# A transformer pair on one core: the low parts of the context stream's weights subtracted on VectorE instead of GpSimd

## The chip, the core and the metric

The kernel runs on one core of a Trainium2 chip. The time is the device time of one execution in microseconds (us). Before the change three runs took 2317.82, 2322.16 and 2325.53 us, a median of 2322.16 us. The kernel is one long program of some 38,000 instructions on five engines: TensorE (PE in the profile; its weight loads are PEld), VectorE (DVE), ScalarE (ACT), GpSimd (POOL) and the queue that issues transfers (SP).

## The reference, cut to what matters

Two model blocks follow each other on 256 tokens of width 1024, batch 1. The first is a mixing block; the second has two layers with a second stream of 256 context tokens. The parts that this case speaks of:

```
def first_block(x, ...):                       # "block 1"
    xn = rms_norm(x, norm_mix); proj = xn @ w_in
    y_r = rwkv7_group(proj[..., :R_COLS], ...)      # a recurrent state over the tokens, 8 heads of 64x64
    y_n = nsa_group(proj[..., R_COLS:], ...)        # sparse attention
    h = x + concatenate([y_r, y_n]) @ w_out
    h = h + swiglu(rms_norm(h, norm_ffn), w_gate, w_up, w_down)
    return rms_norm(h, norm_final)

def second_block(x, c, ctx, c_ctx, w_ada, ...):
    h_x, h_c = x, ctx                               # two streams
    for l in range(2):
        mod_x = silu(c) @ w_ada[l] + b_ada[l]       # the "ada" products; mod_c likewise from c_ctx
        h_x = half_ffn(h_x, ..., ffn1_up[l], ffn1_down[l])
        h_c = half_ffn(h_c, ..., ffn1_up[l], ffn1_down[l])
        ... attention of three kinds over both streams, w_out, a second half_ffn ...
    return rmsnorm(h_x, final_g)
```

The context stream of the second block's first layer (`h_c`) needs nothing of the first block. Its feed-forward part and the ada products can therefore be worked on while block 1 is under way.

## The kernel before, in words

All large products are in float32 by way of two parts. A weight piece of 128x1024 numbers (512 KB) is loaded as `r`. ScalarE casts it to a reduced format, the high part `h` (line 356). A subtraction then gives the low part `l = r - h` (line 357). The activations are held as a high and a low part too (`yh`, `yl`, or `hh`, `hl` inside a feed-forward part). `gemm` adds three products per slice into PSUM: first, for all slices, weight-high times activation-high (line 364) and weight-high times activation-low (line 365), then, for all slices, weight-low times activation-high (line 368). So the low part of a piece is wanted only after 16 products with its high part, in a piece of 8 slices.

The class `Stream` holds the buffers of one such supply of weights: so many raw pieces, so many `h` and `l`. Three of them matter. `s1` and `s` feed block 1 and the main stream. `st_c` (name "sc", 3 raw, 2 `h`, 2 `l`) feeds the context stream: the context's first feed-forward part and then its mixer, and the raw pieces of the ada products (line 1168, which need no parts). Only `st_c` is made with `eng=g`, so only its subtractions run on GpSimd; the others run on VectorE. The tile names tell the streams apart on TensorE: PSUM tiles of the context and ada work are named `f` while block 1 runs, those of block 1 are named `m` and `o`.

Block 1 has long chains of small steps. Those that the prediction speaks of, in order of time: the sparse attention (lines 732 to 796, about 160 to 300 us); the preparation of the recurrence (lines 829 to 926, 300 to 345 us); the products `LT`, `QB`, `AK`, `QK` (lines 951 to 955, to 374 us); a triangular solve written as 31 pairs of dependent VectorE instructions (`tm` at line 977, `TW` at line 978, 374 to 412 us); the recurrence over 8 chunks of tokens (lines 994 to 1055, 423 to 502 us), in which each chunk needs the state `SB` of the one before (L1023, then `U` at L1024, then L1031 and L1032, then the new `SB` at L1041; GpSimd scales the old state at L1040); and the end (lines 1064 to 1085), where a mean, a variance with a power on GpSimd (`hr`, line 855) and a gate follow each other, and then the first pieces of `w1o` are loaded (called "the tail" below).

The order of the instructions on each engine is not written out by hand. The program is built with a scheduler that plays a timeline of its own and puts every engine's instructions into one fixed queue in the order in which that timeline finds them ready. Each engine then works through its queue in order. So the context and ada products are spread between block 1's steps on TensorE by this planner.

Of the kernel before, what the change touches and what calls it, by code (L numbers as in the profile page):

```python
# [15 lines left out]
OP = mybir.AluOpType  # L16
# [249 lines left out]
def build(tc, A, O, dbg=(), stop=None):  # L266
    nc = tc.nc
    v, s, g, te, sy = nc.vector, nc.scalar, nc.gpsimd, nc.tensor, nc.sync
    es = ExitStack()

    def pool(name, bufs=1, space=None, side=None, stack=es, **k):
        if space is not None:
            k["space"] = space
        if side is not None:
            k["side"] = side
        return stack.enter_context(tc.tile_pool(name=name, bufs=bufs, **k))
# [7 lines left out]
    def tl(p, shape, dt=F32, tag="", bufs=None, name=None):  # L284
        k = {}
        if tag:
            k["tag"] = tag
        if bufs:
            k["bufs"] = bufs
        return p.tile(list(shape), dt, name=uniq(name or tag or "t"), **k)  # L290
# [8 lines left out]
    f32 = lambda a: a.bitcast(F32)  # L299
# [31 lines left out]


    class Stream:
        def __init__(self, name, nr, nh, side=None, stack=es, eng=None, parts=None):
            self.nr = nr
            self.raw = pool(name + "r", nr, side=side, stack=stack)
            self.h = pool(name + "h", nh, side=side, stack=parts or stack)
            self.l = pool(name + "l", nh, side=side, stack=parts or stack)
            self.q = sy
            self.e = eng or v  # L340

        def load(self, src, a, b, i=0):

# [8 lines left out]
        def get(self, src, a, b):  # L352
            r = self.load(src, a, b)
            h = tl(self.h, [128, 1024], F32R, tag="h")[:, 0:a * b].rearrange("p (a b) -> p a b", a=a)
            l = tl(self.l, [128, 1024], F32R, tag="l")[:, 0:a * b].rearrange("p (a b) -> p a b", a=a)
            s.copy(h, r)  # L356
            self.e.tensor_tensor(l, r, f32(h), op=OP.subtract)  # L357
            return h, l

    def gemm(pt, w, m0, m1, xs):  # L360
# [1226 lines left out]
    R = "right"  # L1587
# [4 lines left out]

    rs, rs2 = ExitStack(), ExitStack()
    pad = pool("pada", 1, side=R, stack=rs)
    st_c = Stream("sc", 3, 2, side=R, stack=rs, eng=g, parts=rs2)
    st_c.pad = pad
    e = ExitStack()
    first = []
# [89 lines left out]
    rs = ExitStack()  # L1688
# [75 lines left out]
```

## Time and profile before

| what | value |
|---|---|
| runs | 2317.82, 2322.16, 2325.53 us |
| the profiled execution's own time | 2317.79 us |
| its span, first to last instruction | 2315.6 us |
| TensorE busy | 2215.6 us (96%), weight loads 1935.3 us |
| VectorE, ScalarE, GpSimd busy | 1365.0, 965.7, 361.1 us |
| subtractions of line 357 on VectorE | 467, 1233 ns on average |
| subtractions of line 357 on GpSimd | 80, 2431 ns on average, 194.2 us in all |
| mean granted TensorE clock | 0.979 of 2.4 GHz |

The profiled execution took 2317.79 us, 2.2 us more than its span, and 4.4 us less than the median of the runs. TensorE is busy nearly all the time, so the useful reading is where it is not. The 80 subtractions on GpSimd start between 110.5 and 776.0 us of the span.

### The profile page before, as it was taken

To read this page: it belongs to the slowest core of one execution; us is meant where nothing else is said; L and a number is where in the kernel's file an instruction comes from. 1 tells how busy PE (TensorE), PEld (TensorE's weight loads), DVE (VectorE), ACT (ScalarE), POOL (GpSimd) and SP (SyncE) were. 2 spreads that over 40 slices of the span, in tenths; PEclk is the share of its full clock that TensorE was granted. 3 is DMA by queue.
4 is the path that set the end of the run, shared out by engine and by line. 5 is a ranking of instruction groups with operands and counts; after the bars stand their busy time and mean duration, and the time that the engine had idled before them with its cause. 6 is when DMAs were issued, how large, how long until landed. Compare 5 with 4: busy or idle time off the path is not lost.

```text
span 2315.6 us, 38336 instructions
## 1 busy us (share of the span) xinstructions
PE 2215.6 (96%) x15317; PEld 1935.3 (84%) x15317; DVE 1365.0 (59%) x2442; ACT 965.7 (42%) x1602; POOL 361.1 (16%) x286
## 2 busy tenths in 40 slices
PE   7999988998999899998999999999999999989998
PEld 3687876878999799997878777798888889878998
DVE  4465567348665876667765333357534347776665
ACT  4334432226444555445643222245332325564443
POOL 2025464444010300002010000011000002310000
PEclk9999999999999999999999999999999999999999
DMA  8765544436655245554166434376623235413554
GB/s 312 255 220 191 175 159 143 135 121 215 197 183 176 91 129 167 185 168 144 58 221 228 175 131 167 134 236 210 200 87 97 95 119 170 140 46 122 187 183 127
DMA packets 114929, 376.25 MB, mean 162 GB/s; under 512 B 18464, under 2 KB 24480, under 8 KB 114752
## 3 DMA queue, kind: packets, MB, share of 16 engines
q1 hardware_dynamic: 114752, 373.82, 49.1%
q8 instruction: 120, 1.97, 0.3%
q14 instruction: 57, 0.47, 0.1%
HBM read 372.20 MB, written 1.57 MB: 161 GB/s over the span
## 4 chain that ended last, share of the span: by engine, by line
PE 76%; issue 9%; DVE 7%; DMA 4%; POOL 2%; ACT 1%; SPq 0%; POOLq 0%; DVEq 0%; ACTq 0%
PE m L364 13%; PE m L365 13%; PE m L368 13%; PE f L364 8%; PE f L365 7%; PE f L368 7%; PE f L1168 4%; PE o L1399 2%; DVE l L357 1%; PE f L1389 1%; DMA r<-in_up 1%; ACT h L356 1%; DMA r<-in_ada 1%; DVE tm L977 1%; POOL sa L400 1%
## 5 line engine op out<-in xcount | busy, mean ns | idle before, releaser
L356 ACT CAST h<-r 128x1024 fp32r<-128x1024 f32 (+1 forms) x547 | 570.0, 1043 | 950.4 <-PE m L365 453.9
L357 DVE TENSOR_TENSOR l<-r,h 128x1024 fp32r<-128x1024 f32 (+1 forms) x467 | 575.5, 1233 | 284.1 <-ACT h L356 236.7
L365 PE MATMUL m<-yl,h 128*128 128x256 f32 (+1 forms) x1624 | 441.9, 303 | 3.5 <-DVE yl L437 3.4
L364 PE MATMUL m<-yh,h 128*128 128x256 f32 (+1 forms) x1624 | 441.5, 303 | 1.5 <-ACT yh L436 1.5
L364 PEld LDWEIGHTS m<-yh,h 128*128 128x128 f32 x1624 | 310.1, 192 | 27.3 <-issue 10.4
L365 PEld LDWEIGHTS m<-yl,h 128*128 128x128 f32 x1624 | 310.4, 192 | 21.4 <-DVE yl L437 6.4
L368 PE MATMUL m<-yh,l 128*128 128x256 f32 (+1 forms) x1624 | 258.6, 300 | 0.0
L357 POOL TENSOR_TENSOR l<-r,h 128x1024 fp32r<-128x1024 f32 x80 | 194.2, 2431 | 368.2 <-ACT h L356 234.3
L368 PEld LDWEIGHTS m<-yh,l 128*128 128x128 f32 x1624 | 225.1, 190 | 14.2 <-issue 3.7
L400 POOL TENSOR_TENSOR sa<-sa,sq 128x256 f32<-128x256 f32 x81 | 83.3, 1029 | 873.2 <-ACT sq L396 462.9
L365 PE MATMUL m<-hl,h 128*128 128x256 f32 (+1 forms) x738 | 207.0, 303 | 0.0
L364 PE MATMUL m<-hh,h 128*128 128x256 f32 (+1 forms) x738 | 197.2, 304 | 0.0
L364 PE MATMUL f<-yh,h 128*128 128x256 f32 (+1 forms) x624 | 185.3, 321 | 1.1 <-ACT yh L436 1.1
L365 PE MATMUL f<-yl,h 128*128 128x256 f32 (+1 forms) x624 | 184.1, 319 | 0.0
L365 PEld LDWEIGHTS m<-hl,h 128*128 128x128 f32 x738 | 139.8, 189 | 6.9 <-issue 0.4
L364 PEld LDWEIGHTS m<-hh,h 128*128 128x128 f32 x738 | 135.9, 189 | 11.1 <-issue 2.1
L1549 DVE SCALAR_TENSOR_TENSOR res<-m,mod,res 128x256 f32<-128x256 f32 x176 | 81.0, 479 | 108.0 <-PE m L368 105.5
L364 PEld LDWEIGHTS f<-yh,h 128*128 128x128 f32 x624 | 119.2, 191 | 17.3 <-issue 5.4
L364 PE MATMUL f<-hh,h 128*128 128x256 f32 (+1 forms) x446 | 126.6, 313 | 6.5 <-DVE res L1549 6.3
L368 PE MATMUL m<-hh,l 128*128 128x256 f32 (+1 forms) x738 | 129.9, 302 | 0.0
L365 PE MATMUL f<-hl,h 128*128 128x256 f32 (+1 forms) x446 | 126.6, 306 | 2.4 <-DVE hl L372 2.4
L1168 PE MATMUL f<-r,sc 128*32 128x512 f32 (+1 forms) x640 | 118.3, 573 | 8.4 <-DMA r<-in_ada 7.8
(513 smaller groups left out, 3772.5 us busy)
## 6 DMA issues: line engine op xcount, KB each, us to landing
r<-in_up SPq DMA_DIRECT2D x252, 512.0 KB, 3.6
r<-in_ada SPq DMA_DIRECT2D x144, 512.0 KB, 4.4
r<-in_dn SPq DMA_DIRECT2D x98, 512.0 KB, 3.9
r<-in_w1u SPq DMA_DIRECT2D x44, 512.0 KB, 3.5
r<-in_dn SPq DMA_DIRECT2D x32, 448.0 KB, 3.3
r<-in_w2m SPq DMA_DIRECT2D x24, 512.0 KB, 3.8
r<-in_w2o SPq DMA_DIRECT2D x24, 512.0 KB, 3.4
r<-in_w1d SPq DMA_DIRECT2D x22, 512.0 KB, 3.5
```

What stands on the lines that cost most here:

```text
L356: s.copy(h, r)
L357: self.e.tensor_tensor(l, r, f32(h), op=OP.subtract)
L364: te.matmul(pt, w[0][:, k, m0:m1], xs[k][0], start=k == 0, stop=False)
L365: te.matmul(pt, w[0][:, k, m0:m1], xs[k][1], start=False, stop=False)
L368: te.matmul(pt, w[1][:, k, m0:m1], xs[k][0], start=False, stop=k == n - 1)
L400: g.tensor_tensor(acc, acc, sq, op=OP.add)
L977: v.tensor_mul(tm, TW[:, 0:m, j:j + 1].to_broadcast([128, m, n]), Ls[:, j:j + 1, j + 1:32].to_broadcast([128, m, n]))
L1168: te.matmul(pt[j * 32:j * 32 + 32], adac[:, k], w[j], start=k == 0, stop=k == KD - 1)
L1389: te.transpose(pT[:, b * 128:b * 128 + 128], P[:, b * 128:b * 128 + 128], ident)
L1399: te.matmul(po[j * 64:j * 64 + 64], vals(b // 2, b % 2, kvof(2 * pr + j)), PT[j][:, b], start=b == 0, stop=b == nt - 1)
L1549: v.scalar_tensor_tensor(r, pt[:, i * T:i * T + T], ad[l].M[:, m, d, q:q + 1], r, op0=OP.mult, op1=OP.add)
```

## The change

The subtractions of `st_c` are issued on VectorE, like those of the other streams. The argument that chose the engine goes away. No instruction's shape, type or buffer changes; 80 instructions move from GpSimd's queue to VectorE's.

```diff
     class Stream:
-        def __init__(self, name, nr, nh, side=None, stack=es, eng=None, parts=None):
+        def __init__(self, name, nr, nh, side=None, stack=es, parts=None):
             self.nr = nr
...
             self.q = sy
-            self.e = eng or v
...
             s.copy(h, r)
-            self.e.tensor_tensor(l, r, f32(h), op=OP.subtract)
+            v.tensor_sub(l, r, f32(h))
             return h, l
...
-    st_c = Stream("sc", 3, 2, side=R, stack=rs, eng=g, parts=rs2)
+    st_c = Stream("sc", 3, 2, side=R, stack=rs, parts=rs2)
```

Because the planner places instructions by its own timeline, the queues of the engines come out in another order. Lines after 340 have a number lower by one in the changed kernel (L977 and L978 become L976 and L977, L1023 becomes L1022, L357 becomes L356).

VectorE's queue in the middle of the triangular solve (`tm`, `TW`; `res` is the context stream's residual, `fu`, `ft`, `hl` its activations). Before:

```order
L977 TENSOR_TENSOR tm_2226<-TW_2181,Ls_2178 128x7x18
L978 TENSOR_TENSOR TW_2181<-TW_2181,tm_2226 128x7x18
L1549 SCALAR_TENSOR_TENSOR res_60<-f_4398,mod_11_85,res_60 128x256
L977 TENSOR_TENSOR tm_2229<-TW_2181,Ls_2178 128x8x17
L1549 SCALAR_TENSOR_TENSOR res_60<-f_4412,mod_11_85,res_60 128x256
L978 TENSOR_TENSOR TW_2181<-TW_2181,tm_2229 128x8x17
L1549 SCALAR_TENSOR_TENSOR res_60<-f_4432,mod_11_85,res_60 128x256
L977 TENSOR_TENSOR tm_2232<-TW_2181,Ls_2178 128x8x16
L978 TENSOR_TENSOR TW_2181<-TW_2181,tm_2232 128x8x16
L977 TENSOR_TENSOR tm_2235<-TW_2181,Ls_2178 128x9x15
```

The same place on VectorE in the changed kernel:

```order
L356 TENSOR_TENSOR l_4738<-r_4735,h_4737 128x1024
L976 TENSOR_TENSOR tm_2223<-TW_2181,Ls_2178 128x7x19
L371 TENSOR_TENSOR hl_4720<-ft_4717,hh_4719 128x256
L977 TENSOR_TENSOR TW_2181<-TW_2181,tm_2223 128x7x19
L976 TENSOR_TENSOR tm_2226<-TW_2181,Ls_2178 128x7x18
L977 TENSOR_TENSOR TW_2181<-TW_2181,tm_2226 128x7x18
L976 TENSOR_TENSOR tm_2229<-TW_2181,Ls_2178 128x8x17
L458 SCALAR_TENSOR_TENSOR fu_4768<-ft_4766,f_4741 128x256
L977 TENSOR_TENSOR TW_2181<-TW_2181,tm_2229 128x8x17
L976 TENSOR_TENSOR tm_2232<-TW_2181,Ls_2178 128x8x16
L977 TENSOR_TENSOR TW_2181<-TW_2181,tm_2232 128x8x16
L976 TENSOR_TENSOR tm_2235<-TW_2181,Ls_2178 128x9x15
```

Subtractions of weight pieces now stand between the pairs of the solve: 12 between its first and its last instruction, 15 with those just ahead of it and behind it. The context stream is also further on at the same step of the solve: its PSUM tile is `f_4741` here where it was `f_4398` before.

TensorE's queue in one chunk of the recurrence, from the sixth product with the state on (`m`, `o` are block 1's; `f` is the context stream's fill). Before, its first 12 rows; 40 rows lie between the two L1023:

```order
L1023 MATMUL m_2489<-SB_407_1914,WT_2290 32x128 x4
L1026 MATMUL o_2463<-AR_2009,SB_407_1914 128x32 x4
L1031 MATMUL m_2499<-Vt_2078,Kt_2064 128x128
L365 MATMUL f_4984<-ylc_1018,h_4951 128x256
L364 MATMUL f_4984<-yhc_1017,h_4951 128x256
L365 MATMUL f_4984<-ylc_1018,h_4951 128x256
L364 MATMUL f_4984<-yhc_1017,h_4951 128x256
L365 MATMUL f_4984<-ylc_1018,h_4951 128x256
L364 MATMUL f_4984<-yhc_1017,h_4951 128x256
L365 MATMUL f_4984<-ylc_1018,h_4951 128x256
L364 MATMUL f_4984<-yhc_1017,h_4951 128x256
L365 MATMUL f_4984<-ylc_1018,h_4951 128x256
```

The same chunk on TensorE in the changed kernel, whole:

```order
L1022 MATMUL m_2489<-SB_407_1914,WT_2290 32x128 x4
L1025 MATMUL o_2463<-AR_2009,SB_407_1914 128x32 x4
L1030 MATMUL m_2499<-Vt_2078,Kt_2064 128x128
L1031 MATMUL m_2499<-U_2334,Bt_2050 128x128
L1030 MATMUL m_2499<-Vt_2078,Kt_2064 128x128
L1031 MATMUL m_2499<-U_2334,Bt_2050 128x128
L1030 MATMUL m_2499<-Vt_2078,Kt_2064 128x128
L1031 MATMUL m_2499<-U_2334,Bt_2050 128x128
L1030 MATMUL m_2499<-Vt_2078,Kt_2064 128x128
L1031 MATMUL m_2499<-U_2334,Bt_2050 128x128
L1022 MATMUL m_2514<-SB_406_1913,WT_2290 32x128 x4
```

The fill is gone from this chunk. From the first product of line 994 to the first product of `w1o`, TensorE's queue held 296 context products and 32 ada products before, and holds 44 and 16 now; the others stand earlier, 102 and 12 of them in the solve.

## Rows read from the trace of the kernel before

**Rows 1.** The page's busy times: engine, busy us, share, instructions.
```profile
PE 2215.6 (96%) x15317; PEld 1935.3 (84%) x15317; DVE 1365.0 (59%) x2442; ACT 965.7 (42%) x1602; POOL 361.1 (16%) x286
```

**Rows 2.** Busy us (instructions) of PE, PEld, DVE, ACT, POOL by stretch; clock, DMA.
```profile
100.00:300.00 200.00, 194.49 (x1519) 160.24 (x1518) 108.62 (x236) 83.98 (x182) 82.05 (x44) 1.00 0.61 202
300.00:345.00 45.00, 37.73 (x259) 31.93 (x258) 37.40 (x50) 15.00 (x20) 27.77 (x13) 0.92 0.43 142
345.00:374.00 29.00, 29.00 (x168) 20.74 (x166) 16.21 (x39) 5.19 (x8) 10.14 (x6) 1.00 0.54 161
374.00:423.00 49.00, 37.62 (x279) 34.33 (x277) 36.47 (x82) 12.19 (x16) 22.59 (x10) 0.90 0.48 141
423.00:490.00 67.00, 67.00 (x561) 60.15 (x557) 21.75 (x38) 15.45 (x21) 31.10 (x22) 1.00 0.34 114
490.00:531.00 41.00, 33.70 (x240) 23.02 (x240) 22.46 (x42) 11.91 (x23) 19.73 (x15) 0.95 0.54 187
```

**Rows 3.** The same view of three short stretches with a low clock.
```profile
305.00:312.00 7.00, 5.13 (x25) 5.08 (x25) 6.24 (x12) 4.12 (x5) 2.89 (x1) 0.51 0.37 129
390.40:393.90 3.50, 3.50 (x16) 3.50 (x17) 2.48 (x9) 1.04 (x1) 0.23 (x1) 0.51 0.16 63
407.50:414.40 6.90, 5.86 (x27) 5.86 (x28) 3.62 (x17) 1.45 (x2) 0.00 (x0) 0.51 0.34 84
```

**Rows 4.** TensorE's waits, 100 to 423 us: who, for whom, us, times, longest.
```profile
PE f L364 <- DVE res L1549: 8.1, 4, 4.2
PE f L364 <- DVE fu L459: 3.6, 1, 3.6
PE f L365 <- DVE hl L372: 2.4, 1, 2.4
...
PE f L368 <- POOL l L357: 0.3, 1, 0.3
```

**Rows 5.** The page's groups of line 357: busy us, mean ns | idle before, releaser.
```profile
L357 DVE TENSOR_TENSOR l<-r,h 128x1024 fp32r<-128x1024 f32 (+1 forms) x467 | 575.5, 1233 | 284.1 <-ACT h L356 236.7
...
L357 POOL TENSOR_TENSOR l<-r,h 128x1024 fp32r<-128x1024 f32 x80 | 194.2, 2431 | 368.2 <-ACT h L356 234.3
```

**Rows 6.** Line 357 on VectorE: ns min/median/max, first and last start.
```profile
L357 DVE TENSOR_TENSOR l<-r,h x467: 1078/1219/3101, 18.5 to 2294.1; 128x1024 fp32r<-128x1024 f32 x145, 128x896 fp32r<-128x896 f32 x11
```

**Rows 7.** VectorE in order of time in the solve: start us, us.
```profile
382.43 0.28 DVE L977 TENSOR_TENSOR tm<-TW,Ls 128x110 f32<-128x110 f32 x1
...
385.94 2.38 DVE L977 TENSOR_TENSOR tm<-TW,Ls 128x120 f32<-128x120 f32 x1
```

**Rows 8.** GpSimd in order of time, the same stretch (one of 8 rows).
```profile
385.84 2.35 POOL L357 TENSOR_TENSOR l<-r,h 128x1024 fp32r<-128x1024 f32 x1 [0.41 <-DMA r<-in_up]
```

**Rows 9.** TensorE on PSUM tiles `f` alone: stretch, busy us (instructions), clock, DMA.
```profile
423.00:531.00 108.00, 51.58 (x370) 0.98 0.42 142
```

**Rows 10.** A chunk of the recurrence in order of time.
```profile
489.70 1.08 PE L1026 MATMUL o<-AR,SB 128*128 128x32 f32 x8
489.80 0.69 DVE L1024 TENSOR_TENSOR U<-m,Uv 32x512 f32<-32x512 f32 x1 [1.83 <-PE m L1023]
...
494.67 0.38 PE L1032 MATMUL m<-U,Bt 32*128 32x128 f32 x2
...
495.16 0.87 DVE L1041 TENSOR_TENSOR SB<-st,m 64x256 f32<-64x256 f32 x2 [3.94 <-PE m L1032]
...
497.12 1.06 PE L1023 MATMUL m<-SB,WT 128*32 128x128 f32 x8
```

**Rows 11.** The tail in order of time.
```profile
507.32 1.06 ACT L1067 ACTIVATE sq<-Y 128x1024 f32<-128x1024 f32 x1 [2.94 <-DVE Y L1065]
...
511.77 2.90 POOL L855 TENSOR_TENSOR hr<-hr,mhalf 128x16 f32<-128x16 f32 x1 [13.09 <-DVE hr L854]
...
515.45 1.09 PE L864 MATMUL m<-cst,rx 128*128 128x128 f32 x8 [1.45 <-DVE rx L859]
...
530.70 0.58 PE L364 MATMUL m<-mixh,h 128*128 128x256 f32 x1 [5.85 <-ACT h L356]
```

## The prediction

> **What bounds the kernel now.** I read the page's busy times first. TensorE is busy 96% of the span, VectorE 59%, GpSimd 16% [rows 1]. So the time is TensorE's work, which the change leaves as it is, plus the time in which TensorE has nothing to do or runs at half clock. Only that remainder can move.
>
> The second view is the table by stretch. The subtractions that change engine run mostly under block 1, so I cut that part by its stages. TensorE's idle time is the stretch less PE's busy time: 5.5 us in the attention (100 to 300), 7.3 us in the preparation (300 to 345), none in the products (345 to 374), 11.4 us in the solve (374 to 423), none in most of the recurrence (423 to 490) and 7.3 us in its end and the tail (490 to 531) [rows 2]. That is 31.5 us, of which 24.2 us lie before 423.
>
> Third, the clock. Three stretches before 423 run at 0.51 of 2.4 GHz, that is at the 1.2 GHz level, with 5.13, 3.50 and 5.86 us of TensorE work in them [rows 3]. At full clock that work would take about half, so some 7 us are lost there. Idle time and clock together are 31 us before 423: the ceiling of any gain there.
>
> Fourth, the waits of TensorE before 423. It waited 0.3 us for a subtraction on GpSimd, once. It waited 8.1, 3.6 and 2.4 us for VectorE's `res`, `fu` and `hl` of the context stream [rows 4]. So the subtraction itself is hidden. If GpSimd costs anything, it is by what it does to VectorE.
>
> **The price of one subtraction.** On GpSimd it takes 2431 ns on average, 80 times, 194.2 us [rows 5]. On VectorE the same operation takes 1078 ns at best and 1219 ns in the middle [rows 6]. So VectorE gets 80 x 1.08 = 86 us, at most 80 x 1.22 = 98 us. Most of them fall before 531 us.
>
> **What goes: VectorE held by GpSimd.** In the solve `tm` takes 0.28 us at 382.43 and 2.38 us at 385.94, for shapes that differ by 9% [rows 7]. A subtraction on GpSimd runs from 385.84 for 2.35 us [rows 8]. The VectorE instruction that starts inside it ends with it. There are 8 such subtractions in the solve, so about 8 x 2.0 = 16 us of 36.5 us VectorE busy time there is standing still; I count 15, since one of them came too late in its overlap to cost the full amount.
>
> The Trainium skill states this as a rule ("SBUF — State Buffer", section Who interferes with whom): a VectorE instruction with two SBUF inputs and a GpSimd instruction that reads SBUF exclude each other, and the later one waits until the other has finished. The trace agrees, 2.38 us against 0.28 us. But another page ("Perfetto Trace Analysis", section Optimizing Scalar/DVE Operations) warns that, because the two share a port, moving work between them might not help. By it the gain below would be nothing and the sum would be plus 17 us; the rows decide for a gain, since VectorE stands 2.0 us per collision and needs 1.1 us to do the work itself.
>
> **The solve (374 to 423).** VectorE loses 15 us of standing and gains 15 subtractions (front part), 15 x 1.08 = 16 us, and some 4 us more of `fu`, `ft`, `hl`: 36.5 - 15 + 16 + 4 = 42 us. TensorE's queue gains 102 context and 12 ada products there. The 370 recorded fill instructions of 423 to 531 take 51.58 us, 0.14 us each [rows 9], and an ada product of the queue is two of those. So TensorE's work grows from 37.6 to about 37.6 + 14 + 3 = 55 us. Before, VectorE's chain was the longer; now TensorE's work is, by 13 us. I expect its idle time to fall from 11.4 to 4 us, and the clock loss there (4.7 us of the 7) to go: a gain of 12 us. Bounds: 16 us (all of it), and a loss of 4 us if VectorE's queue stalls. A subtraction in VectorE's queue waits for its cast on ScalarE, on average 236.7 / 467 = 0.5 us today [rows 5]; 15 of them are 7.6 us, which fits under the 13 us. What is queued behind such a wait is the solve itself and `res`, `fu`, `hl`, for which TensorE waits.
>
> **The preparation (300 to 345).** VectorE is busy 37.4 of 45 us and GpSimd 27.8 us, which is some ten subtractions [rows 2]. About eight would come to VectorE (9 us) against some 8 us of standing that go. Since `hl` and `res`, for which TensorE waited, are held less, I take a gain of 4 us with the clock, from a loss of 6 to a gain of 8. **The attention (100 to 300)** has 5.5 us idle, and more fill between its steps; I take nothing, from -5 to +4.
>
> **What comes: a recurrence without fill.** The queue behind line 994 holds 44 + 16 fill products where it held 296 + 32. In recorded instructions that is 44 + 32 = 76 of 370, so 294 x 0.14 = 41 us of fill have moved to before 423. Moving costs nothing as such. But the recurrence is a chain, and what hid its waits is gone. In the chunk shown, `U` (0.69 us from 489.80) is hidden by L1026, which ends at 490.78. After the last L1032 (494.67) `SB` takes until 496.03, and L1023 needs it: 495.16 + 0.87 - (494.67 + 0.38) = 1.0 us, with the hand-over 1.2 us [rows 10]. Four of the seven chunks have nothing there now: 5 us (3 to 7). In one chunk two subtractions for the mixer stand in VectorE's queue ahead of `SB`, right after the last ada loads; I add 2 us (0 to 5).
>
> **The tail.** Fill hid the waits for the mean and for `sq` (about 1.5 and 2 us, an estimate: 1.06 us of ScalarE for `sq`, and VectorE steps as wide as `U` with its 0.69 us), and part of the power on GpSimd: `hr` takes 2.90 us, and only 1.45 us of the wait for it showed [rows 11]. Without fill I get 1.5 + 2 + 4 = 7.5 us where 1.45 us showed: a loss of 6 us (3 to 9), and 1 us at the first `w1o` piece, where 5.85 us of waiting for its load remain. More idle time in the tail should bring the half clock there: 3 us (0 to 7). After 531 us TensorE is nearly full, and the moved subtractions there lie under its work; I take nothing.
>
> **The sum.** Gains 12 + 4 = 16 us; losses 5 + 2 + 6 + 1 + 3 = 17 us. On the profiled execution's 2317.8 us that is 2319 us; on the median of the runs, 4.4 us higher, 2323 us. With every term at its better end it would be 22 us faster (gains 16 + 8 + 4, losses 3 + 0 + 3 + 0 + 0); with every term at its worse end 44 us slower (4 + 6 + 5, and 7 + 5 + 9 + 1 + 7). They will not all fall on one side.
>
> **The rivals.** First, **the locks pay in full**: VectorE answers sooner in every stretch before 423, and TensorE's 31 us there shrink to about 12, while the recurrence and the tail cost 10. That is 9 to 15 us faster, 2307 to 2313 us. For it: all the large waits of TensorE there name VectorE [rows 4]. Against: fill that is used early is missing later.
>
> Second, **VectorE's queue becomes the bound**: subtractions stand in it in a fixed place and wait for casts, which wait for loads and for TensorE to free the two `h` buffers; each of about 40 of them in the attention, the preparation and the solve holds it for 0.5 us beyond its own 1.08 us, so 20 us of waits, half of them in chains that TensorE waits for. It decides where VectorE was already full, at 300 to 345. That takes 10 us off the gain, and with the losses it is 10 to 20 us slower, 2333 to 2343 us. Against: VectorE has 59% load overall [rows 1]. The warning of the page "Perfetto Trace Analysis" in the Trainium skill, read as no gain at all, comes to a time in the same range.
>
> Third, **nothing happens**, because TensorE never waited for GpSimd's subtraction: 2322 us. Against: the queues do change, by hundreds of rows.
>
> **How the numbers follow.** A measurement here tells about 0.3% (7 us) from no change. Forecast (the sum) 0.35, nothing happens 0.09, locks in full 0.27, queue the bound 0.29. The forecast and the third rival lie within 0.3%: 0.44 same; 0.27 faster, 0.29 slower. The forecast's own range is 2316 to 2330 us. The range for 8 in 10 takes in most of both other cases: 2307 to 2340 us.
>
> **What would show it.** Right: no VectorE `tm` over 1 us; TensorE idle under 6 us in the solve; 1 us of idle time per late chunk of the recurrence, which takes about 60 us instead of 79; 13 us or more idle in the tail. Wrong: idle time of TensorE before 423 that stays above 24 us, with waits for `l` or for `res` behind an `l`; or a tail that shows no more waiting than before.

## The result: slower, by 0.7 to 0.8%

Four runs of the changed kernel took 2336.8, 2338.68, 2340.07 and 2345.07 us, a median of 2339.38 us against 2323.27 us for the kernel before: a ratio of 1.0076 (95% interval 1.0050 to 1.0102). Timed again later beside other kernels (e16 below) it was 1.0068 (1.0055 to 1.0081). The forecast of 2323 us, no change that can be measured, was wrong; the time fell at the far end of the range.

The profiled execution took 2340.07 us. The page's busy times, the group of line 356 (357 before) and the mean clock, to be held against [rows 1, 5]:

```profile
PE 2232.3 (95%) x15317; PEld 1951.7 (83%) x15317; DVE 1389.8 (59%) x2522; ACT 967.3 (41%) x1602; POOL 167.8 (7%) x206
...
L356 DVE TENSOR_TENSOR l<-r,h 128x1024 fp32r<-128x1024 f32 (+1 forms) x547 | 667.5, 1221 | 337.7 <-ACT h L355 289.7 <-PE m L367 17.7 <-PE f L367 9.9
...
core 0: 2338.3 us, clock 0.969
```

VectorE has the 80 subtractions at 1.22 us each and is hardly busier (1389.8 us against 1365.0, where 80 x 1.22 us make 98), because GpSimd no longer makes it stand still. But TensorE, with the same 15317 instructions, is busy 16.7 us longer. Work that is the same and takes longer is a matter of the clock: 0.969 here, 0.979 before.

The table by stretch says where; columns as in [rows 2], cut at the changed kernel's own stages (preparation, solve, then from the first product of line 993 on, with a cut where the clock fell and one at the end of the recurrence):

```profile
320.00:366.00 46.00, 39.67 (x295) 34.72 (x294) 39.13 (x61) 16.91 (x25) 7.84 (x3) 0.93 0.51 179
...
391.00:444.50 53.50, 49.04 (x405) 44.39 (x404) 40.68 (x102) 19.70 (x26) 0.00 (x0) 0.97 0.64 206
444.50:483.90 39.40, 36.31 (x322) 30.42 (x322) 14.30 (x28) 5.29 (x8) 4.37 (x8) 1.00 0.43 148
483.90:521.40 37.50, 32.72 (x148) 26.72 (x145) 6.86 (x13) 0.58 (x1) 3.02 (x5) 0.50 0.05 15
521.40:546.00 24.60, 16.02 (x47) 9.55 (x46) 11.93 (x22) 6.62 (x14) 10.34 (x11) 0.57 0.13 48
```

The solve's idle time is 53.5 - 49.0 = 4.5 us where it was 11.4. But from 483.9 to 546 us TensorE runs almost throughout at the 1.2 GHz level (0.50 and 0.57); in the same stages before, the table showed 1.00 and 0.95 [rows 2]. Just before the clock fell at 483.9 us it had waited 3.02 us, because two subtractions of the mixer's weights stood in VectorE's queue ahead of the new state `SB`:

```profile
480.10 2.53 DVE L356 TENSOR_TENSOR l<-r,h 128x1024 fp32r<-128x1024 f32 x2 [4.91 <-ACT h L355]
...
482.66 0.87 DVE L1040 TENSOR_TENSOR SB<-st,m 64x256 f32<-64x256 f32 x2
...
483.68 1.68 PE L1022 MATMUL m<-SB,WT 128*32 128x128 f32 x8 [3.02 <-DVE SB L1040]
```

The place is not fixed. In another profiled execution of the same kernel (e16, its slowest, 2351.1 us) the clock was low already in the first chunk, from 449.3 us on: 0.57 from 449.2 to 474.4 us, with TensorE busy throughout. What TensorE waited for in the first execution between 444 and 548 us (who, for whom, us, times, longest):

```profile
PE m L1022 <- DVE SB L1040: 6.4, 4, 3.0
PE m L863 <- DVE rx L858: 4.1, 1, 4.1
PE f L422 <- DVE sq L420: 2.3, 1, 2.3
PE m L848 <- ACT sq L1066: 2.0, 1, 2.0
PE m L1063 <- DVE Y L1054: 1.4, 1, 1.4
```

One whole chunk of the recurrence in order of time, the answer to [rows 10]:

```profile
492.33 1.89 PE L1022 MATMUL m<-SB,WT 128*32 128x128 f32 x8 [1.12 <-DVE SB L1040]
494.15 1.92 PE L1025 MATMUL o<-AR,SB 128*128 128x32 f32 x8
494.26 0.68 DVE L1023 TENSOR_TENSOR U<-m,Uv 32x512 f32<-32x512 f32 x1 [2.07 <-PE m L1022]
...
499.14 0.63 PE L1031 MATMUL m<-U,Bt 32*128 32x128 f32 x2
499.88 0.87 DVE L1040 TENSOR_TENSOR SB<-st,m 64x256 f32<-64x256 f32 x2 [4.94 <-PE m L1031]
...
500.90 1.46 PE L1022 MATMUL m<-SB,WT 128*32 128x128 f32 x6 [1.12 <-DVE SB L1040]
```

The wait for `SB` is 1.12 us, as forecast; the one longer wait, 3.02 us, is that of the chunk with the two subtractions. VectorE's `SB` takes 0.87 us as before. But the product of L1025 takes 1.92 us where it took 1.08, and the chunk 8.57 us.

Last, the solve's pairs (ns minimum/median/maximum), the answer to [rows 7]: no `tm` is over 0.30 us any more.

```profile
L976 DVE TENSOR_TENSOR tm<-TW,Ls x31: 181/267/303, 391.2 to 434.6; 128x126 f32<-128x126 f32 x3, 128x30 f32<-128x30 f32 x2, 128x56 f32<-128x56 f32 x2, 128x78 f32<-128x78 f32 x2
```

### The profile page after: what moved, and what is told of

It reads as the page before. It is cut to its first block, busy times and chain, and to the rows that moved or that the text cites. A ratio compares the mean times of both kernels' runs of the same rounds, so it can differ in the third digit from the quotient of the medians.

```text
span 2338.3 us, 38319 instructions
## 1 busy us (share of the span) xinstructions
PE 2232.3 (95%) x15317; PEld 1951.7 (83%) x15317; DVE 1389.8 (59%) x2522; ACT 967.3 (41%) x1602; POOL 167.8 (7%) x206
## 4 chain that ended last, share of the span: by engine, by line
PE 79%; issue 9%; DVE 5%; DMA 4%; ACT 2%; POOL 1%; SPq 0%; POOLq 0%; DVEq 0%; ACTq 0%
PE m L363 13%; PE m L364 13%; PE m L367 13%; PE f L363 8%; PE f L367 7%; PE f L364 7%; PE f L1167 4%; PE o L1398 2%; DMA r<-in_ada 1%; DVE l L356 1%; PE f L1388 1%; ACT h L355 1%; DMA r<-in_up 1%; POOL sa L399 1%; PE f L1268 1%
## 5 line engine op out<-in xcount | busy, mean ns | idle before, releaser
L356 DVE TENSOR_TENSOR l<-r,h 128x1024 fp32r<-128x1024 f32 (+1 forms) x547 | 667.5, 1221 | 337.7 <-ACT h L355 289.7
L364 PEld LDWEIGHTS f<-yl,h 128*128 128x128 f32 x624 | 118.8, 190 | 7.8
```

The lines of the kernel that those rows point to most:

```text
L356: v.tensor_sub(l, r, f32(h))
L364: te.matmul(pt, w[0][:, k, m0:m1], xs[k][1], start=False, stop=False)
```

## The experiments

Theory T1: the planner, with subtractions on VectorE, uses the fill up before the recurrence; TensorE, left with short products and waits, runs there at 1.2 GHz, and that is the loss. Rival R1: the subtractions in VectorE's queue delay the chains. Rival R2: the loss lies in the later stages.

Every execution comes with its span and mean granted clock. From them, the time at half clock is 2 x (1 - clock) x span, and span x clock is the span counted in full-speed time. The clock has three digits, so the first is good to about 2 us, the second to 1 us. Medians over each kernel's runs:

| kernel | us | ratio to before, 95% interval | half clock us | span x clock us |
|---|---|---|---|---|
| before (23 to 29 runs in each of four sets) | 2320.3 to 2323.4 | | 88 to 93 | 2273 to 2274 |
| after (4 runs) | 2339.4 | 1.0050 to 1.0102 | 143 | 2266 |
| e1 narrow extra products | 2335.0 | 1.0037 to 1.0085 | 131 | 2269 |
| e2 every second on GpSimd | 2325.6 | 1.0005 to 1.0037 | 123 | 2262 |
| e3 last 47 on GpSimd | 2341.8 | 1.0071 to 1.0118 | 129 | 2274 |
| e4 first 33 on GpSimd | 2329.6 | 1.0030 to 1.0057 | 130 | 2262 |
| e5 wide extra products | 2329.6 | 1.0007 to 1.0055 | 112 | 2273 |
| e6 e4 and wide extra products | 2325.5 | 1.0003 to 1.0037 | 98 | 2275 |
| e7 e2 and extra products in the tail | 2327.0 | 0.9994 to 1.0029 | 119 | 2267 |
| e8 less fill, GpSimd (one run) | 2311.7 | (work left out) | 185 | 2218 |
| e9 the same again | 2304.1 | (work left out) | 173 | 2216 |
| e10 less fill, VectorE | 2329.0 | (work left out) | 202 | 2225 |
| e11 mixer's 14 on VectorE | 2325.8 | 1.0006 to 1.0028 | 95 | 2275 |
| e12 two of three on GpSimd | 2324.4 | 0.9996 to 1.0027 | 109 | 2267 |
| e13 after, 8 more ada steps | 2333.4 | 1.0012 to 1.0063 | 117 | 2268 |
| **e14 after, 16 more ada steps** | **2318.5** | **0.9965 to 0.9992** | 93 | 2271 |
| e15 before, 16 more ada steps | 2341.1 | 1.0066 to 1.0093 | 103 | 2287 |
| e16 after again (5 runs) | 2338.6 | 1.0055 to 1.0081 | 140 | 2267 |

The first two rows hold the size of it. In full-speed time the change gains 7 us. It pays with 50 us more at half clock, half of which, 25 us, is lost. This sum halves idle time at half clock as well, so it is good to a few us only; TensorE's own busy time grew by 16.7 us in the profile. A stage table below shows one execution, not the median: those of e4, e9 and e10 are the fastest of their kernels, those of e2 and e13 among the three fastest of twelve, that of e7 the slowest.

That half is what half clock costs can be seen inside single kernels, whose executions differ. The 12 runs of e5 go from 2314.5 us (83 us at half clock) to 2348.2 us (145 us); a straight line through them rises 0.50 us per us of half clock. For e13 it is 0.49, from 2317.3 us at 102 us to 2349.4 us at 164 us. These two vary most; the other kernels with eleven or twelve runs give 0.37 to 0.53, but for e11, whose half clock varies by 9 us only and shows no slope. The Trainium skill ("TensorE: Matmul & The Clock Gate", section Terms) prices throttled time at the share of clock pulses withheld, here one half; these two slopes agree.

**e1, narrow extra products** in the waits, read by nobody, after the change (shortened):

```diff
+    for p in range(4): te.matmul(pd[:, w], Bt[t][o, w], U[t][o, w], ...)   # each chunk, behind L1031
+    for _ in range(3): te.matmul(pd, bom, flat(Y)[:, 512:1024], ...)       # tail, ahead of sq
+    for _ in range(4): te.matmul(pd, bom, flat(sq)[:, 512:1024], ...)      # tail, behind L848
```

> Extra TensorE products whose results nobody reads, in the waits of the recurrence (4 of 128 columns a chunk) and of the tail (3 and 4 of 512 columns); all 80 subtractions stay on VectorE. If the loss is the half clock over 61 us of recurrence and tail (theory T1), the granted clock from 445 to 546 rises to 0.85 or more, the stretch of 101.6 us falls to 82 to 90, and the time to 2319 to 2330. If the subtractions in VectorE's queue are what delays the chains (rival R1), the clock is beside the point: the extra products only add their 3 to 8 us and the time is 2339 to 2348. If the loss lies after 546 (rival R2), 2337 to 2343.

Not settled: 2335.0 us lies between the theories. The stretches (end of the solve to the second chunk; to the mean; to `w1o`):

```profile
444.30:470.80 26.50, 26.47 (x146) 23.93 (x146) 4.00 (x8) 2.34 (x4) 1.23 (x2) 0.57 0.16 60
470.80:524.40 53.60, 51.76 (x375) 44.12 (x374) 16.39 (x31) 3.63 (x5) 7.03 (x10) 0.80 0.26 89
524.40:546.60 22.20, 16.56 (x62) 8.75 (x62) 10.83 (x20) 6.50 (x14) 10.03 (x10) 0.94 0.18 59
```

The tail kept its clock (0.94) and took 22.2 us, 5.7 us less than the same part of the changed kernel's profile (27.9 us), with more work in it. But now the clock was low from 445 us on, ahead of the first extra product (466.3 us). TensorE had stood idle 2.53 us for a transfer up to 442.7 us and 0.54 us more up to 444.3. Behind that it was busy for 26.47 of 26.50 us, and the clock did not stay up: it rose at 461.8 us and fell again at 465.3, without a gap.

```profile
444.30:461.80 17.50, 17.47 (x95) 15.69 (x96) 2.67 (x5) 1.76 (x3) 0.00 (x0) 0.51 0.24 91
461.80:465.30 3.50, 3.50 (x28) 3.19 (x28) 0.00 (x0) 0.59 (x1) 0.00 (x0) 0.99 0.00 0
465.30:472.10 6.80, 6.80 (x36) 6.13 (x36) 1.81 (x4) 0.20 (x1) 1.23 (x2) 0.50 0.00 0
```

**e2, e3, e4, splits of the subtractions** (shortened):

```diff
-            v.tensor_sub(l, r, f32(h))
+            (g if n % 2 else v).tensor_tensor(l, r, f32(h), op=OP.subtract)    # e2; n counts the stream's pieces
+            (g if n >= 33 else v)...    # e3
+            (g if n < 33 else v)...     # e4
```

> Every second subtraction of the context stream back on GpSimd (40 of 80). The fill products that are queued between the second chunk and the mean of the tail are 182 instead of 26 (226 before). T1: the clock stays at 2.4 GHz there as before the change, the time is 2317 to 2327. R1: half of the subtractions, half of the loss, 2329 to 2334. R2: between, 2326 to 2335.

> The first 33 subtractions on VectorE, the last 47 on GpSimd: 158 fill products between the second chunk and the mean. T1: clock nearly as before the change in the recurrence, 2318 to 2328. R1: the VectorE queue is free of them from the middle of the preparation on, where the recurrence and solve stand, 2322 to 2328; this run alone does not part T1 from R1, it does so together with the next.

> The mirror of it: the first 33 subtractions on GpSimd, the last 47 on VectorE. 58 fill products between the second chunk and the mean. T1: little fill, most of the half clock stays (30 to 55 us of it between 480 and 550), 2331 to 2340. R1, with 47 of 80 on VectorE and most of them in the solve and recurrence: 2332 to 2338. If instead the attention's stretch, with VectorE's queue there, is what costs, this one is at 2323 and the one before it at 2339.

e2 came out as T1 had it, e4 slightly better than T1 had it. e3 lies above what T1 and R1 had; only the third way, named with e4, had the order of the two (e3 at 2339 us, e4 at 2323): that VectorE's queue in the attention's stretch is what costs. e3 and e4 have the same half clock, so the 12 us between them are something else, and the solve shows a part of it (`tm` in e3, then in e4):

```profile
L981 DVE TENSOR_TENSOR tm<-TW,Ls x31: 186/274/2355, 389.7 to 426.5; 128x126 f32<-128x126 f32 x3, 128x30 f32<-128x30 f32 x2, 128x56 f32<-128x56 f32 x2, 128x78 f32<-128x78 f32 x2
```

```profile
L981 DVE TENSOR_TENSOR tm<-TW,Ls x31: 178/267/304, 378.4 to 422.2; 128x126 f32<-128x126 f32 x3, 128x30 f32<-128x30 f32 x2, 128x56 f32<-128x56 f32 x2, 128x78 f32<-128x78 f32 x2
```

Of the 62 `tm` and `TW`, those over 1 us number 8 in e3, with 8 GpSimd subtractions in the solve; 4 with 4 in e2; 6 with 6 in e12; none with none in e4 and after; 8 with 7 before. TensorE's idle time in the solve is 8.1 us in e3 and 3.1 in e4, and from its end to the start of the recurrence 3.6 and 0.5 us. So the mutual hold that the prediction took from [rows 7, 8], and from the Trainium skill ("SBUF — State Buffer", section Who interferes with whom), is real, and the idle time that goes with it is about 8 of the 12 us. The rest, and with it the third way, stays open.

e2 also shows a limit of T1. Ahead of its solve, behind a wait of 2.7 us, TensorE ran at half clock for 27 us, though 55 of the 87 instructions there, 14.0 of 26.3 us, were the context stream's fill:

```profile
360.40:387.70 27.30, 26.32 (x87) 18.29 (x88) 13.77 (x40) 3.47 (x5) 3.35 (x3) 0.50 0.46 142
```

So fill between other products does not always bring the clock back.

**e5, e6, e7, wide extra products.** On all 128 rows, one a chunk: `te.matmul(pu, Bt[t][:, 0:128], Vt[t], ...)` behind L1031, with the tail's of e1. e5 has it on the changed kernel, e6 on the split of e4; e7 has the tail's alone on the split of e2.

> All 80 subtractions on VectorE. Extra products without a reader again, but wide ones on all 128 rows: one of 512 columns a chunk in the wait for the new state (6 chunks), and 3 and 4 of 512 columns in the tail, about 0.9 us each. Span times mean clock was 2266 us after the change and is expected at 2265 to 2271 here. If half clock is the loss (T1) and filling the waits keeps the clock up, half-clock time falls from 145 us to 85 to 105 and the time to 2311 to 2324. If the clock falls anyway, already with the solve just ahead (as it did at 445 us with the narrow products), 125 to 145 us of half clock remain and 2330 to 2340. If VectorE's queue is the loss (R1): 2340 to 2350, whatever the clock does.

> The same extra products, with the first 33 subtractions on GpSimd and the last 47 on VectorE. Span times mean clock was 2261.5 us with that split, 10 us less than before the change (2272), at 128 us of half clock. T1: half-clock time 85 to 100 us, 2308 to 2318, faster than both kernels. If the clock falls anyway: 2325 to 2332.

> Every second subtraction on GpSimd, which leaves fill in the recurrence, and the wide extra products in the tail alone. T1: the 17 us of half clock in and behind the tail of that split (2325.6 us) go, 6 to 8 us: 2316 to 2321. If the clock is not what costs in the tail, the extra products add 0 to 3 us: 2325 to 2329.

Recurrence and tail of e5:

```profile
464.60:514.00 49.40, 47.94 (x339) 34.56 (x338) 16.36 (x31) 3.63 (x5) 7.03 (x10) 0.89 0.29 96
514.00:536.10 22.10, 16.57 (x63) 8.78 (x63) 10.89 (x21) 6.50 (x14) 9.93 (x10) 0.94 0.17 60
```

The clock stayed up (0.89 and 0.94), the two stages took 71.5 us where they took 86.4 us in the profile after, and the time fell by 10 us although only work was added: against R1, which had 2340 to 2350. T1's number was too good (2311 to 2324), and in e6 too (2308 to 2318): extra products are not free. A wide one in a chunk took 1.5 us (six, 8.9 us), not 0.9. They brought span x clock up by 6 us in e5 and by 13 us in e6; in e6 that ate most of the 16 us that 32 us less half clock gave. And other half clock came: in e5's profile the two stages have 45 us less of it than after the change, the whole execution 29. e7 gained nothing, as the other outcome named there had it (2325 to 2329): the half clock of its tail went (4.8 us left in the profile), other half clock came, 119 us in all against 123. Where that comes from was not settled.

**e8, e9, e10, less fill.** The last two of six groups of the context's feed-forward part are left out: `range(len(CGROUPS) - 2)`. e8 and e9 are the kernel before so cut, e10 the changed one.

> The kernel before, all 80 places of the subtraction on GpSimd, with the last two of the six groups of the context's first feed-forward part left out, so that no fill product is queued in the recurrence or the tail (0 instead of 226 and 34). T1: the clock falls there without any subtraction on VectorE: 35 us or more of half clock between the products with TT and the first of w1o (3.7 us before). If the subtractions on VectorE bring it about, 10 us or less. The time tells nothing here, work is missing.

> The kernel before without the last two groups of the context's first feed-forward part, subtractions on GpSimd, now timed, as the partner of the next. One execution of it showed half clock over 82 us of recurrence and tail and took 2311.7 us. Expected: 2307 to 2316, half-clock time 170 to 195 us.

> The same work left out, all subtractions on VectorE. With no fill in the recurrence in either of the two, the clock can't be lost by the change once more. T1: the sign turns; the time is 4 to 14 us below its GpSimd partner (the 7 us of span times clock that the change gained, or more), with half-clock time within 20 us of it. R1 (VectorE's queue delays the chains, whatever the clock): 5 to 15 us above its partner.

Recurrence and tail of the kernel before, then of e8, both with GpSimd's subtractions:

```profile
440.00:504.70 64.70, 64.70 (x540) 56.20 (x540) 21.34 (x39) 12.75 (x17) 29.28 (x20) 1.00 0.35 115
504.70:530.70 26.00, 18.70 (x106) 10.80 (x105) 17.39 (x32) 8.53 (x16) 14.68 (x13) 0.93 0.56 199
```

```profile
440.30:500.70 60.40, 53.41 (x272) 46.07 (x272) 11.09 (x21) 1.79 (x3) 11.26 (x14) 0.53 0.05 18
500.70:529.10 28.40, 19.16 (x51) 10.67 (x51) 12.83 (x24) 6.64 (x14) 10.35 (x11) 0.56 0.14 48
```

This is the clearest single reading. Half of TensorE's instructions are gone from the recurrence (272 instead of 540), it has not one subtraction on VectorE, and it takes 60.4 instead of 64.7 us. Fill in the recurrence was nearly free, because without it the clock is low (0.53 against 1.00). R1 is not needed for the loss there. Its share in the profile after the change is the one wait of 3.02 us that two subtractions made; whether the clock would have stayed up at that place without them, no run shows.

The pair e9 and e10 went against T1 as I had put it: with no fill in the recurrence of either, I expected VectorE to win by 4 to 14 us, and it lost by 25. The sign is that of R1, which had 5 to 15 us. Their recurrences are indeed alike (429.5 to 490.0 and 445.9 to 506.4). The difference lies ahead of it; solve and start of the recurrence in e9, then in e10:

```profile
372.40:412.80 40.40, 29.17 (x200) 17.43 (x198) 26.83 (x78) 4.40 (x6) 8.30 (x4) 0.78 0.63 195
412.80:429.50 16.70, 15.66 (x126) 12.41 (x125) 2.65 (x5) 3.78 (x6) 0.90 (x1) 0.91 0.53 190
429.50:490.00 60.50, 53.46 (x272) 46.16 (x272) 11.08 (x21) 1.62 (x3) 11.10 (x14) 0.53 0.05 18
```

```profile
390.70:423.20 32.50, 12.62 (x46) 1.77 (x42) 18.25 (x67) 2.46 (x3) 0.00 (x0) 0.61 0.68 214
423.20:445.90 22.70, 21.63 (x112) 20.47 (x113) 2.64 (x5) 2.34 (x4) 0.50 (x1) 0.50 0.02 4
445.90:506.40 60.50, 53.45 (x273) 46.08 (x273) 11.09 (x21) 1.17 (x2) 6.90 (x12) 0.53 0.00 1
```

With less fill to begin with, VectorE's faster answers use it up one stage sooner: the solve has 46 TensorE instructions left instead of 200 and TensorE stands idle 20 of 32.5 us, at a mean clock of 0.61 and then 0.50. What R1 says does not show: e10 comes to its solve 18.3 us later than e9 with 165 more fill instructions done, and only 2.8 us of that is more idle time of TensorE; the solve itself is shorter. So T1 had to be put wider: the fill runs dry earlier, at whatever stage, and the stages behind pay in idle time and in clock.

**e11 and e12.** e11 has only the last 14 subtractions (`n < 66` on GpSimd) moved, e12 two of three on GpSimd.

> The kernel before, with only the last 14 subtractions, those of the context's mixer, on VectorE; the queues of block 1 stay as before. If a part of the loss lies there (R2: lag rose by 7 us between the first w1o product and the end): 2325 to 2331. T1, with the clock lost in the recurrence and tail alone: within 4 us of the kernel before, 2317 to 2325.

> Two of three subtractions on GpSimd; 182 fill products between the second chunk and the mean of the tail, as with every second one. T1: the recurrence keeps its clock, half-clock time 100 to 125 us, span times clock between 2262 and 2273: 2318 to 2327. Faster than the kernel before only if the clock holds in the products of LT, QB, AK, QK too, where the split by halves had half clock for 27 us.

e11 is 4 us slower than before (1 to 7), at the same half clock: a part of R2 may be true. Against it stands e4, which has these 14 on VectorE too and takes 1783.7 us from the first `w1o` product to the end where the kernel before took 1784.9. e12, with its fill kept, is not told from the kernel before.

**e13 to e16, real fill put back.** More of the ada products, which later stages would have made, are issued behind the context's feed-forward part; nothing is added or left out:

```diff
-        fill(max(0, 40 - 8 * len(EARLY) - done[0]))
+        fill(max(0, 48 - 8 * len(EARLY) - done[0]))   # e13; 56 in e14 and, on the kernel before, in e15
```

> The changed kernel, with 8 steps more of the ada products (taken from later stages, no work added) made behind the context's first feed-forward part: 44 ada and 30 context products between the second chunk and the mean instead of 12 and 26, none in the tail. The queues up to the recurrence stay as they are. T1: half clock from the second chunk to the mean falls from 34 us to under 10; with the tail's 24 us left, the time is 2318 to 2328. R1: 2336 to 2342, the VectorE queue has not changed. A third way: the ada pieces (1 MB a step) come too late in the recurrence, TensorE waits on transfers there, and it is 2330 to 2345.

> The same with 16 steps: 22 ada products in the tail as well. T1: little half clock in the recurrence and the tail, total 90 to 110 us, and the idle 16 us there filled: 2300 to 2318, faster than both kernels. R1: 2336 to 2342. Transfers too late: 2325 to 2345.

> The kernel before with the same 16 steps more. Its recurrence is full already and its tail gets 2 more products only; T1: 2312 to 2324, no or a small gain. If it gains as much as e14 does over the changed kernel, the gain there is that of the later stages and not of the clock.

> The changed kernel as it is. 2335 to 2343, half-clock time 130 to 150 us, span times mean clock 2264 to 2268 us.

Recurrence and tail of e13, then of e14:

```profile
460.50:513.60 53.10, 51.65 (x395) 33.72 (x394) 14.68 (x33) 2.13 (x4) 6.62 (x11) 0.97 0.62 202
513.60:542.50 28.90, 18.62 (x53) 11.20 (x51) 15.39 (x26) 8.64 (x16) 10.36 (x11) 0.58 0.38 132
```

```profile
464.60:517.80 53.20, 51.55 (x395) 33.76 (x394) 14.65 (x32) 2.13 (x4) 6.57 (x11) 0.97 0.61 201
517.80:546.00 28.20, 22.84 (x98) 9.14 (x96) 10.78 (x25) 7.23 (x15) 10.11 (x11) 0.94 0.73 251
```

e13's recurrence keeps its clock (0.97) and, with 71 more instructions, is 5 us shorter than the 58.5 us after the change; its tail, which got none, stays at 0.58. Its median missed T1's range (2318 to 2328) and lies in that of late transfers (2330 to 2345); but in its profiled execution (2319.1 us) TensorE waited for a transfer of these pieces 0.4 us in these two stages. Its runs scatter most (97 to 164 us of half clock). e14 fills the tail too, 0.94, and there the 16 steps cost nothing: 81.4 us for both stages against 86.4. Its time is half a microsecond above T1's range. It is faster than the kernel before (2318.5 us, 0.22% with an interval of 0.08% to 0.35%) and 20 us faster than e16 beside it. The same 16 steps in the kernel before make it 18 us slower, which I had not expected. Both gain 22 us at the end, where these products no longer stand (e14, then e15):

```profile
1264.90:2309.30 1044.40, 1028.80 (x6516) 913.78 (x6514) 575.12 (x925) 415.62 (x636) 65.02 (x66) 0.99 0.42 136
```

```profile
1284.90:2332.60 1047.70, 1030.37 (x6516) 915.45 (x6514) 574.16 (x925) 415.74 (x636) 66.32 (x66) 0.99 0.42 136
```

Before the change that part took 1070.2 us, after it 1067.1. But e15 has no room earlier: its recurrence and tail are full, the steps go to the stage behind them, which had 0.8 us idle, and everything is later.

## Why the prediction was wrong, point by point

- **What bounds it, and the hold of VectorE by GpSimd: right.** No `tm` over 0.30 us, one subtraction 1.22 us, the solve's idle time 4.5 us where I said 4.
- **The gain before 423: right in size.** The first product of line 993 starts 21.4 us later (444.5 against 423.1 us), with 284 more fill instructions done by then; at 0.14 us [rows 9] these are 40 us, an estimate. That leaves a gain of 18 us; I had 16.
- **Fill out of the recurrence: right as a mechanism.** 1.12 us of wait a chunk, idle time from 444.5 to 546 us 3.1 + 4.8 + 8.6 = 16.5 us against 7.3 before: 9 us more, where my terms (5, 2, 6 and 1) made 14. The waits for `SB` (6.4 us for 5 + 2) and in the tail (1.4, 2.0 and 4.1 us for 1.5, 2 and 4) came as forecast. The wait for the first `w1o` piece did not: 0.3 us, where I left the 5.85 us of [rows 11] and added 1. So the tail has 8.7 us of idle time where I named 13 or more as a sign.
- **"More idle time in the tail should bring the half clock there: 3 us (0 to 7)": this term failed.** It was 61 us of half clock (483.9 to 521.4 and 524.9 to 548.7 us), in the recurrence as well as the tail, where there were 7. TensorE's instructions on block 1's tiles took 63.6 (`m`) and 10.9 us (`o`) there instead of 47.2 and 7.6: 20 us. The recurrence took 73.7 us from the first product of line 993 to the mean; my sign of being right was about 60. I looked for the clock only where idle time is long, and priced the one long wait in the recurrence as a wait; I did not ask what the recurrence's own products do to the clock when they are alone. Here it fell behind that wait and stayed low for 37.5 us, of which TensorE worked 32.7. e8 shows that they lose it with GpSimd too, e14 that it stays up with real fill between them.
- **After 531, nothing: wrong by 7 us.** The lag grows from 15.4 us at the first `w1o` product to 22.7 us. Most of it is at the hand-over around 800 us: TensorE waits there for `sa`, a sum on GpSimd, 5.3 us instead of 2.0, and has 20 us of half clock instead of 14. e11 leaves room for a few us from the mixer's subtractions, e4 none. Why that wait grew was not settled.
- **The rivals.** Queue the bound had the right time for the wrong reason: the trace after shows no wait of TensorE for one of these subtractions, and one of 3.02 us for an `SB` held by two of them; e5 and e14 win time with the same queue on VectorE. Locks in full: the locks did pay, before 423.

The account in the trace: -18 before the recurrence; +9 idle and +20 clock in the recurrence and tail, and 5 more; +7 later. Of the 5, some 4 are the 85 fill instructions left there, which took 15.4 us, or 0.18 us each instead of 0.14, an estimate; 1 has no place. That is +23 us, and the spans differ by 22.7.

## What to carry to other kernels

Work that fills waits is a stock: what makes it go faster in one stage takes it from the next, so a gain in front must be booked together with the stage in which the stock ends. Where a chain of short products is left alone, as here at 0.50 to 0.57 of the clock (after, e8, e9, e10), price its TensorE work at 1.2 GHz too, not its waits only; e2 shows that some fill is no guarantee. An edit that frees an engine may pay only when something real is moved into the room that it makes, as in e14.

## What the runs showed that I had not expected

- The clock was low, and fell a second time, while TensorE had no gap: 26.47 of 26.50 us busy at a mean of 0.57, 120 of the 146 instructions block 1's own (e1). Its first fall there came behind waits of 2.53 and 0.54 us.
- 268 instructions more in the recurrence cost 4.3 us (60.4 against 64.7 us), and with them the granted clock is 1.00 where it is 0.53 without (e8).
- One kernel's executions differ by up to 34 us (e5) with no change in the program, nearly all of it by time at half clock.
